# Seven block products in place of eight in a SwiGLU step, and a last stage laid out by tokens

## The chip, the cores and the metric

The kernel runs on one core of one Trainium2 chip. The metric is the device time of one execution in microseconds (us), here the median of three runs of the kernel before. The core has five engines with queues of their own: TensorE (PE in the profile, its weight loads PEld), VectorE (DVE), ScalarE (ACT), GpSimd (POOL) and SyncE (SP, which issues most DMAs).

## What is computed

One decoder layer on 512 tokens of width 1024, in float32: a SwiGLU half step, a mixer (attention beside a state-space model), a second SwiGLU half step, a gated embedding and a final norm. The change lies in the last three:

```python
h = h + 0.5 * swiglu(rmsnorm(h, g_ffn2), w1_b, w3_b, w2_b)
gate = sigmoid(rmsnorm(h, g_ple) @ w_ple_gate)
h = h + gate * (p @ w_ple_proj)
return rmsnorm(h, g_final)
# swiglu(x, w1, w3, w2) = (silu(x @ w1) * (x @ w3)) @ w2 ; w1, w3: 1024x2816, w2: 2816x1024
```

## The kernel before

The residual stream X lies transposed: eight tiles of 128 features x 512 tokens. A float32 product is made of three: every operand is split into hi (a cast to the type that PE reads) and lo = value - hi, and `mm3` (L235 to 238) issues hi*hi, lo*hi and hi*lo. So each weight piece of 128x512 passes through three engines before PE sees it: SP loads it into one of five raw buffers (`wdma`, L141), ACT casts it to hi and DVE subtracts (`split_w`, L152 to 168); the subtraction done, the raw buffer is free and the next load may start. A norm needs no pass of its own: the operand is X times the gain, and the factor 1/rms is applied behind the product (`Norm`, L254 on; its `chain` sums the squares on PE, takes the power on POOL and spreads the result by PE).

The work is a list of units of two steps each. `run` (L205) emits for each step, in this order: the hi casts of the next unit's weights, due evictions, chains, due posts, the lo subtractions, the step's matmuls. Every engine executes its queue in the order of emission, so this order is the schedule. `extra` asks for the conversion of a piece ahead of its unit.

The second FFN (`ffn_units`, L340; `U2`) has its 2816 hidden features in 22 tiles of 128, in three parts of 7, 7 and 8. For each tile there is one unit for the gate product (w1) and one for the linear product (w3): 8 blocks of the width x 3 matmuls with 512 tokens, 48 matmuls in the tile. Behind them `gate_a`, `gate_b`, `lin_a`, `lin_b`, `lin_c` (L348 to 368) make the hidden tile on DVE and ACT, with the tanh form of the sigmoid, and split it. After each part come eight w2 units that add the part's share onto X.

The projection of p (`proj_units`, L1222) is made in the mixer, as 8 tiles of features x tokens. The gate stage (`gate_units`, L1263) goes by output features: eight tiles m, and each in two halves of 256 tokens, so that the first half's final norm (`final_chain`, L1317) can run while the second half multiplies. Each unit has 24 matmuls with 256 tokens moving; behind them come the product with 1/rms, a tanh, the product with the projection, the sum onto X and a square. Twelve of the sixteen gate weight pieces are converted early, beside U2's units from the twentieth from the end on (L1418). After the last matmul `final_chain` sums the squares on PE, takes the power on POOL, spreads it over the partitions by PE, scales X by the gains into output tiles and sends them, six DMAs for the second half.

Of the kernel before, what the change touches and what calls it, by code (L numbers as in the profile page):

```python
# [23 lines left out]
PREP = 5  # L24
FEW = 3
# [5 lines left out]
OUT = [[(0, 1), (2, 3), (4, 5), (6, 7)], [(0,), (1, 2), (6,), (3, 4), (7,), (5,)]]  # L31
# [7 lines left out]
G_FFN1, G_MIX, G_FFN2, G_PLE, G_FINAL, G_ATTN, G_SSM, B_GLU = 0, 8, 16, 24, 32, 40, 44, 48  # L39
# [3 lines left out]
def hybrid_trunk_kernel(ctx: ExitStack, tc: tile.TileContext, xT, pT, w13a, w2a, w13b, w2b, wqk, wv, ws, wf,  # L43
                        wglu, wout, wgate, wproj, cols, bf, ssm_s, ssm_bc, dskip, outT, dbg=None):
# [48 lines left out]
    colt = const.tile([128, 52], F32, name="colt")  # L93
# [24 lines left out]
    qsel = [const.tile([128, L], F32R, name=f"qsel{j}") for j in range(2)]  # L118
    kcum = [const.tile([128, L], F32R, name=f"kcum{j}") for j in range(2)]
# [4 lines left out]
    class Unit:  # L124
# [6 lines left out]

        def w(self, c, n=1):
# [5 lines left out]
    wseq, raws = [], {}  # L138
    dma_at = [0]

    def wdma():  # L141
        j = dma_at[0]
        if j >= len(wseq):
            return
        dma_at[0] += 1
        u, i = wseq[j]
        n = u.srcs[i].shape[-1]
        w = pool.tile([128, 512], F32, name=nm("wraw"), tag="wraw", bufs=RAWS)
        nc.sync.dma_start(w[:, 0:n], u.srcs[i])
        raws[(id(u), i)] = w  # L150

    def split_w(u, i):  # L152
# [35 lines left out]
    def convert(u, nxt, h):  # L188
# [3 lines left out]
        if nxt is not None:  # L192
            res = [(nxt, i) for i in range(len(nxt.srcs)) if nxt.parts[i] is None and (i == h or last)]
        return res + [(v, i) for hh, v, i in u.extra if hh == h]

    def order_weights(units):
        seen = set()
        for u, nxt in zip(units, units[1:] + [None]):
            for h in range(len(u.steps)):
                for v, i in convert(u, nxt, h):  # L200
                    if (id(v), i) not in seen:
                        seen.add((id(v), i))
                        wseq.append((v, i))

    def run(units):  # L205
        while dma_at[0] < RAWS:
            wdma()
        for ui, u in enumerate(units):
# [3 lines left out]
            for h, step in enumerate(u.steps):  # L212
# [42 lines left out]
    class Norm:  # L255
# [52 lines left out]
        def chain(self, strided=False, wait=0):  # L308
# [12 lines left out]
            yield  # L321
            ps = bank()
# [899 lines left out]
    def proj_units(pp):  # L1222
# [270 lines left out]
    while chains:  # L1493
        advance(chains)
# [84 lines left out]
```

## Time and profile before

| | |
|---|---|
| median of 3 runs | 1009.3 us (1009.05 to 1009.88) |
| the profiled execution | 1009.63 us |
| its span, first to last instruction | 1007.9 us |
| busy: PE / DVE / ACT / POOL | 99% / 65% / 42% / 8% of the span |
| second FFN's parts 2 and 3, gate and linear tiles | 701.26 to 777.42 and 815.50 to 902.54 us |
| gate stage, then tail | 946.07 to 996.05, then to 1007.90 us |

Times in rows count from the span's start. A row's duration runs from an instruction's start to its end; those of one engine overlap, so the pace of an engine is read from the distance between two starts. "x2" behind a row of the timeline means two instructions merged, whose time is that of both together. POOL's durations are rough. An arrow names the output, then the inputs; buffer numbers are left out.

### The profile page before, as it was taken

To read this page: it belongs to the slowest core of one execution; us is meant where nothing else is said; L and a number is where in the kernel's file an instruction comes from. 1 tells how busy PE (TensorE), PEld (TensorE's weight loads), DVE (VectorE), ACT (ScalarE), POOL (GpSimd) and SP (SyncE) were. 2 spreads that over 40 slices of the span, in tenths; PEclk is the share of its full clock that TensorE was granted. 3 is DMA by queue.
4 is the path that set the end of the run, shared out by engine and by line. 5 is a ranking of instruction groups with operands and counts; after the bars stand their busy time and mean duration, and the time that the engine had idled before them with its cause. 6 is when DMAs were issued, how large, how long until landed. Compare 5 with 4: busy or idle time off the path is not lost.

```text
span 1007.9 us, 13796 instructions
## 1 busy us (share of the span) xinstructions
PE 996.2 (99%) x4980; PEld 838.5 (83%) x4980; DVE 655.1 (65%) x1297; ACT 420.7 (42%) x799; POOL 83.8 (8%) x84
## 2 busy tenths in 40 slices
PE   9999999999999999999999999999999999999996
PEld 7888888888878889887888888888888888888896
DVE  6668788767745565889987965543545347655465
ACT  6333233332244444469995543322333224434232
POOL 0440000001000001004651000000000000000000
PEclk9999999999999999999999999999999999999998
DMA  6423333223345323211212223233232334533102
GB/s 210 147 94 83 110 103 94 87 82 106 100 103 127 95 93 83 62 66 64 85 53 84 88 90 105 85 92 115 86 105 81 109 104 150 164 94 95 32 7 78
DMA packets 58244, 96.06 MB, mean 95 GB/s; under 512 B 10224, under 2 KB 17008, under 8 KB 58176
## 3 DMA queue, kind: packets, MB, share of 16 engines
q1 hardware_dynamic: 57920, 94.63, 31.0%
q8 instruction: 39, 0.64, 0.3%
q0 software_dynamic: 256, 0.56, 0.2%
q14 instruction: 29, 0.24, 0.1%
HBM read 91.89 MB, written 2.10 MB: 93 GB/s over the span
## 4 chain that ended last, share of the span: by engine, by line
PE 91%; DVE 5%; ACT 1%; issue 1%; DMA 1%; POOL 0%; SPq 0%; POOLq 0%; ACTq 0%; DVEq 0%
PE ps L236 29%; PE ps L238 29%; PE ps L237 28%; PE ps L1457 1%; PE ps L1093 1%; DVE rot L75 1%; DVE wlo L75 1%; DVE rc L75 1%; PE ps L324 1%; PE ps L1139 1%; PE ps L316 0%; PE ps L1138 0%; DMA x<-xT 0%; DVE qkhl L75 0%; PE ps L642 0%
## 5 line engine op out<-in xcount | busy, mean ns | idle before, releaser
L236 PE MATMUL ps<-xhl,whi 128*128 128x512 f32 x816 | 320.3, 393 | 0.0
L238 PE MATMUL ps<-xhl,whi 128*128 128x512 f32 x816 | 317.8, 389 | 0.0
L237 PE MATMUL ps<-xhl,wlo 128*128 128x512 f32 x816 | 317.7, 389 | 0.0
L160 ACT CAST whi<-wraw 128x512 fp32r<-128x512 f32 x324 | 195.9, 608 | 240.0 <-PE ps L238 176.9
L75 DVE TENSOR_TENSOR wlo<-wraw,whi 128x512 fp32r<-128x512 f32 x324 | 216.9, 675 | 5.8 <-ACT whi L160 5.5
L238 PEld LDWEIGHTS ps<-xhl,whi 128*128 128x128 f32 x816 | 153.2, 188 | 32.5
L236 PEld LDWEIGHTS ps<-xhl,whi 128*128 128x128 f32 x816 | 153.2, 188 | 31.8 <-issue 1.0
L237 PEld LDWEIGHTS ps<-xhl,wlo 128*128 128x128 f32 x816 | 153.3, 188 | 31.1
L236 PE MATMUL ps<-h,whi 128*128 128x512 f32 x352 | 137.3, 390 | 0.0
L238 PE MATMUL ps<-h,whi 128*128 128x512 f32 x352 | 137.0, 389 | 0.0
L237 PE MATMUL ps<-h,wlo 128*128 128x512 f32 x352 | 137.0, 389 | 0.0
L78 DVE SCALAR_TENSOR_TENSOR x<-ps,x 128x512 f32<-128x512 f32 x48 | 33.2, 692 | 95.1 <-PE ps L238 95.1
L78 DVE SCALAR_TENSOR_TENSOR t<-ps,rbc 128x512 f32<-128x512 f32 x44 | 30.4, 690 | 75.9 <-PE ps L238 75.9
L238 PEld LDWEIGHTS ps<-h,whi 128*128 128x128 f32 x352 | 66.1, 188 | 13.8
L237 PEld LDWEIGHTS ps<-h,wlo 128*128 128x128 f32 x352 | 66.1, 188 | 13.7
L236 PEld LDWEIGHTS ps<-h,whi 128*128 128x128 f32 x352 | 66.1, 188 | 13.5
L75 DVE TENSOR_TENSOR t<-ps,rbc 128x512 f32<-128x512 f32 x44 | 30.4, 691 | 71.1 <-PE ps L238 65.0
L81 ACT ACTIVATE th<-t 128x512 f32<-128x512 f32 x44 | 27.8, 632 | 91.0 <-DVE t L75 91.0
L364 ACT CAST h<-t 128x512 fp32r<-128x512 f32 x44 | 27.4, 622 | 80.9 <-DVE t L75 80.9
L320 POOL TENSOR_TENSOR rc<-ms,mhalf 128x4 f32<-128x4 f32 x6 | 8.0, 1338 | 519.6 <-DVE ms L319 519.6
L1085 POOL TENSOR_SCALAR lg<-lg,rs 128x128 f32<-128x128 f32 (+3 forms) x32 | 37.8, 1195 | 97.9 <-issue 78.7
L81 ACT ACTIVATE xhl<-x,colt 128x512 fp32r<-128x512 f32 x32 | 23.0, 725 | 48.1 <-DVE x L78 41.0
(256 smaller groups left out, 1185.0 us busy)
## 6 DMA issues: line engine op xcount, KB each, us to landing
wraw<-w13b SPq DMA_DIRECT2D x88, 256.0 KB, 2.9
wraw<-w13a SPq DMA_DIRECT2D x84, 256.0 KB, 2.8
wraw<-w2a SPq DMA_DIRECT2D x32, 256.0 KB, 2.7
wraw<-w2b SPq DMA_DIRECT2D x32, 256.0 KB, 2.7
wraw<-wqk SPq DMA_DIRECT2D x16, 256.0 KB, 2.8
wraw<-wout SPq DMA_DIRECT2D x16, 256.0 KB, 2.8
wraw<-wgate SPq DMA_DIRECT2D x16, 256.0 KB, 2.9
wraw<-w2a SPq DMA_DIRECT2D x16, 192.0 KB, 2.4
```

The lines of the kernel that those rows point to most:

```text
L75: V.tensor_tensor(out, a, b, op)
L78: V.scalar_tensor_tensor(out, a, s, b, op0, op1)
L81: S.activation(out, in_, f, **kw)
L160: S.copy(hi[:, 0:n], w[:, 0:n])
L236: T.matmul(ps, lh, rh, start=start, stop=False)
L237: T.matmul(ps, ll, rh, start=False, stop=False)
L238: T.matmul(ps, lh, rl, start=False, stop=stop)
L324: T.matmul(ps[:, i * 128:(i + 1) * 128], rc[:, i:i + 1].to_broadcast([128, 128]), ident, start=True, stop=True)
L364: S.copy(hl[:, 0, :], box["t"])
L1085: G.tensor_scalar(x, x, rs[h2][:, j:j + 1], None, MUL)
L1093: T.transpose(ps[:, j * 128:(j + 1) * 128], lg[h2][:, j * 128:(j + 1) * 128], ident)
L1139: T.matmul(po[:, j * 128:], vv, pl, start=False, stop=j == 3)
```

## The change

- In the second FFN, tiles 0 to 2 stay as they are (`PLAIN`). For each of the 19 others (`quick_units`) the two weight matrices are taken as a 2x2 block matrix, gate and linear by the two halves of the width, and X times gain as 2x2 blocks, halves of the width by halves of the tokens. Seven block products (of 4 blocks x 3 matmuls, 256 tokens moving) replace eight. Their stationary operands are the four raw pieces or sums of them; POOL makes four sums a tile, ACT casts and DVE subtracts seven operands of 128x512. The sums stand in buffers that attention has left (`spare`, `maskp`). The moving operands are X's halves and four combinations of them that `halves` makes once, on ACT, POOL and DVE, beside the plain tiles.
- The seven products are added up in three halves of two PSUM banks. Four intermediate sums are copied out by ACT (`p1`, `p5`, `u2`, `u3`) before the next product is added on. What follows (`gate_a` to `hid_b`) takes ten operations on DVE, ACT and POOL, two of them products with 1/rms on POOL (on DVE in the last tile of each part).
- The operands are taken five products ahead (`AHEAD`). A quick unit has seven steps; its loads wait for the raw buffers of the tile before, which POOL's third sum and DVE's subtractions free (`used`).
- The projection and the gate stage go by tokens: the activations are stationary (128 tokens), the weights move (512 output features). X is turned by PE (`turn`, four transposes for each half of a token tile). 1/rms is a column then and enters as the tanh's scale; the squares are summed by ACT's accumulator, and the final norm needs no product. Three token tiles leave as 512 KB each; the last half tile is made in two pieces (`last`) and leaves in two DMAs.
- The gate weights' subtractions stand on POOL, and twelve are converted beside the last eight w2 units. The final gains come by two DMAs on POOL's queue (`g_load`).

```diff
...
+PLAIN = (3, 0, 0)
...
+    rings = {"w": [], "k": []}
+    SIZE = {"w": RAWS, "k": 1}
     def wdma():
...
+        while dma_at[0] < len(wseq):
+            u, i = wseq[dma_at[0]]
+            ring = "k" if isinstance(u, Quick) and i == 3 else "w"
+            done = rings[ring]
...
+            if ring == "k":
+                w = spare(3)
+            else:
+                w = pool.tile([128, 512], F32, name=nm("wraw"), tag="wraw", bufs=RAWS)
+            nc.sync.dma_start(w[:, 0:n], u.srcs[i])
+            raws[(id(u), i)] = w
+    def used(u, i):
+        ring, j = where[(id(u), i)]
+        rings[ring][j] = True
+        wdma()
...
+            (G.tensor_tensor if u.alloc is not None else tt)(lo[:, 0:n], w[:, 0:n], raw32(hi[:, 0:n]), SUB)
+            used(u, i)
...
+    HT = L // 2
+    def halves(nrm, goff):
+        nrm.ta, nrm.tb = [None] * 4, [None] * 4
+        for _ in range(2):
+            yield
+        for k in range(4):
...
+            act(xa, X[k], AF.Copy, scale=colt[:, goff + k:goff + k + 1])
...
+            G.tensor_tensor(ta[:, 0:HT], xa[:, HT:], xa[:, 0:HT], SUB)
...
+            for _ in range(4):
+                yield
+            for t, dst in ((ta, nrm.ta), (tb, nrm.tb)):
+                hl = g4([128, 2, L], F32R, "xth")
+                S.copy(hl[:, 0, :], t)
+                dst[k] = hl
+                defer(1, lambda t=t, hl=hl: tt(hl[:, 1, :], t, raw32(hl[:, 0, :]), SUB))
+    def quick_units(nrm, w13, fs, hid, before):
+        A21, A22, A11, A12 = range(4)
+        KINDS, AHEAD = 7, 5
+        total = KINDS * len(fs)
+        tens = [Quick([w13[f, wi][:, c * 512:(c + 1) * 512] for wi, c in ((1, 0), (1, 1), (0, 0), (0, 1))]) for f in fs]
+        ops = {}
+        def first_sum(q):
+            G.tensor_tensor(spare(0), q.raw(A21), q.raw(A22), ADD)
+        def take(j):
+            n, i = divmod(j, KINDS)
+            q = tens[n]
+            def f():
+                src = (lambda: q.raw(A11), lambda: spare(0), lambda: maskp, lambda: q.raw(A12), lambda: spare(1), lambda: spare(2),
+                       lambda: q.raw(A22))[i]()
...
+                S.copy(hi, src)
+                ops[j] = hi, lo
+                if i == 0:
+                    G.tensor_tensor(maskp, spare(0), q.raw(A11), SUB)
+                elif i == 2:
+                    G.tensor_tensor(spare(1), q.raw(A11), q.raw(A21), SUB)
+                    used(q, A21)
+                    used(q, A11)
+                elif i == 3:
+                    G.tensor_tensor(spare(2), q.raw(A12), maskp, SUB)
+                elif i == 6 and n + 1 < len(fs):
+                    first_sum(tens[n + 1])
+                def rest():
+                    tt(lo, src, raw32(hi), SUB)
+                    if i == 3:
+                        used(q, A12)
+                    elif i == 6:
+                        used(q, A22)
+                return rest
+            return f
+        def moving(i, k, w):
+            lower, upper = slice(0, HT), slice(HT, L)
+            x, y = nrm.hl[k], nrm.hl[k + 4]
+            src, ts = ((x, lower), (nrm.ta[k], lower), (nrm.ta[k], upper), (y, lower), (nrm.tb[k], lower), (y, upper),
+                       (nrm.tb[k], upper))[i]
+            return src[:, w, ts]
+        before[-2].behind.extend((q, i) for q in tens for i in range(4))
+        before[-2].hooks.setdefault(1, []).append(lambda: first_sum(tens[0]))
+        for h, js in ((0, (0, 1)), (1, (2, 3, 4))):
+            before[-1].hooks.setdefault(h, []).extend(take(j) for j in js)
+        units = []
+        for n, f in enumerate(fs):
+            box = {}
+            def product(i, n=n, box=box):
+                def g(u):
+                    if i < 2:
+                        box[i] = bank()
+                    out = box[0][:, 0:HT] if i in (0, 2, 4, 6) else box[1][:, HT:] if i in (1, 5) else box[1][:, 0:HT]
+                    hi, lo = ops.pop(n * KINDS + i)
+                    for k in range(4):
+                        ks = slice(k * 128, k * 128 + 128)
+                        first = k == 0 and i < 2
+                        T.matmul(out, hi[:, ks], moving(i, k, 0), start=first, stop=False, skip_group_check=i > 1)
+                        T.matmul(out, lo[:, ks], moving(i, k, 0), start=False, stop=False, skip_group_check=i > 1)
+                        T.matmul(out, hi[:, ks], moving(i, k, 1), start=False, stop=k == 3, skip_group_check=i > 1)
+                return g
+            def p1(box=box):
+                box["t"] = tmp(base="t1")
+                S.copy(box["t"][:, 0:HT], box[0][:, 0:HT])
+            def p5(box=box):
+                box["u"] = tmp(base="t3")
+                S.copy(box["u"][:, 0:HT], box[1][:, HT:])
+            def u2(box=box):
+                S.copy(box["t"][:, HT:], box[0][:, 0:HT])
+            def u3(box=box):
+                S.copy(box["u"][:, HT:], box[0][:, 0:HT])
+            last = f == fs[-1]
+            MULT = tt if last else (lambda o, a, b, op: G.tensor_tensor(o, a, b, op))
+            def gate_a(box=box, MULT=MULT):
+                t = box["t"]
+                tt(t, box[1], t, ADD)
+                MULT(t, t, nrm.r, MUL)
+            def lin_a(box=box):
+                u = box["u"]
+                tt(u[:, HT:], u[:, HT:], u[:, 0:HT], ADD)
+            def gate_b(box=box):
+                box["h"] = tmp(base="th")
+                act(box["h"], box["t"], AF.Tanh, scale=0.5)
+            def gate_c(box=box, MULT=MULT):
+                stt(box["t"], box["h"], 1.0, box["t"], ADD, MUL)
+                MULT(box["t"], box["t"], nrm.r, MUL)
+            def lin_b(box=box):
+                h, t = box["h"], box["t"]
+                stt(h[:, HT:], box["u"][:, HT:], 0.5, t[:, HT:], MUL, MUL)
+                stt(h[:, 0:HT], box[0][:, 0:HT], 0.5, t[:, 0:HT], MUL, MUL)
+            def hid_a(box=box, f=f):
+                hl = g4([128, 2, L], F32R, "h")
+                S.copy(hl[:, 0, :], box["h"])
+                hid[f] = hl
+            def hid_b(box=box, f=f):
+                tt(hid[f][:, 1, :], box["h"], raw32(hid[f][:, 0, :]), SUB)
+            d = (0, 0, 0, 1, 1) if last else (0, 1, 2, 3, 4)
+            u = Unit([], [product(i) for i in range(KINDS)],
+                     [(0, 0, p1), (1, 0, p5), (2, 0, u2), (4, 0, u3), (5, 0, gate_a), (5, 0, lin_a)]
+                     + [(6, e, fn) for e, fn in zip(d, (gate_b, gate_c, lin_b, hid_a, hid_b))])
+            for i in range(KINDS):
+                j = n * KINDS + i + AHEAD
+                if j < total:
+                    u.hooks[i] = [take(j)]
+            units.append(u)
+        return units
...
+                if f - part[0] >= n_plain:
+                    units += quick_units(nrm, w13, list(part)[n_plain:], hid, units[-2:])
+                    break
...
+                    for t in (a, a + 1):
+                        ts = slice(t * 128, t * 128 + 128)
+                        box[t] = bank()
                         for k in range(2):
-                            mm3(box[mi], *u.w(mi * 2 + k), phl[k][:, 0, :], phl[k][:, 1, :], k == 0, k == 1)
+                            mm3(box[t], phl[k][:, 0, ts], phl[k][:, 1, ts], *u.w(k * 4, 4), k == 0, k == 1)
...
+        class Tile:
...
+            def turn(self, c):
+                ps = bank()
+                for j in range(4):
+                    T.transpose(ps[:, j * 128:(j + 1) * 128], X[c * 4 + j][:, self.t * 128:self.t * 128 + 128], ident)
+                return ps
+            def gate(self, ps, w):
+                th = tmp(base="gt")
+                act(th[:, 0:w], ps, AF.Tanh, scale=nrm.rc[:, 4 + self.t:5 + self.t])
+                return th
+            def add(self, th, px, c0, w):
...
+                o = self.o[:, c0:c0 + w]
+                stt(th[:, 0:w], th[:, 0:w], 1.0, pp[self.t][:, c0:c0 + w], ADD, MUL)
+                tt(o, th[:, 0:w], px, ADD)
+                act(th[:, 0:w], o, AF.Square, scale=1.0 / 32.0, accum_out=self.ss[:, self.n:self.n + 1])
...
+            def rms(self):
...
+                V.tensor_scalar(ms, ss[:, self.n - 1:self.n], ss[:, self.n - 2:self.n - 1], EPS, ADD, ADD)
+                G.tensor_tensor(rf, ms, mhalf[:, 0:1], ALU.pow)
...
+            def out(self):
+                for c in range(2):
+                    o = self.o[:, c * 512:(c + 1) * 512]
+                    stt(o, o, self.rf, gfb[c], MUL, MUL)
+                nc.sync.dma_start(y_out[self.t * 128:self.t * 128 + 128, :], self.o)
...
+        def products(u_of, ps, t, c, k0, k1, w0=0, w=512):
+            ts = slice(t * 128, t * 128 + 128)
+            for k in range(k0, k1):
+                xh, xl = nrm.pair(k)
+                hi, lo = ws_[c, k // 2].w((k % 2) * 4, 4)
+                mm3(ps[:, 0:w], xh[:, ts], xl[:, ts], hi[:, w0:w0 + w], lo[:, w0:w0 + w], k == 0, k == KD - 1)
...
+        def last():
+            tl = tiles[3]
+            px = tl.turn(1)
+            pss = [bank(), bank()]
             for i in range(2):
+                products(None, pss[i], 3, 1, 0, KD, i * 256, 256)
+                if i == 0:
+                    G.tensor_tensor(tl.o[:, 0:512], tl.o[:, 0:512], gfb[0], MUL)
+                th = tl.gate(pss[i][:, 0:256], 256)
+                tl.add(th, px[:, i * 256:i * 256 + 256], 512 + i * 256, 256)
+            tl.rms()
+            rows = y_out[384:512, :]
+            o = tl.o
+            stt(o[:, 512:1024], o[:, 512:1024], tl.rf, gfb[1], MUL, MUL)
+            nc.sync.dma_start(rows[:, 512:1024], o[:, 512:1024])
+            act(o[:, 0:512], o[:, 0:512], AF.Copy, scale=tl.rf)
+            nc.sync.dma_start(rows[:, 0:512], o[:, 0:512])
+        return units, load, last
...
-    chain_at(u_g[0], n4.chain(wait=1))
-    chain_at(u_g[KD], final_chain(acc5, sqs[0], 0, 3))
+    chain_at(U2[0], halves(n3, G_FFN2))
+    chain_at(u_g[0], n4.chain(wait=4, halved=True))
+    u_g[0].starts.append(g_load)
     for j in range(12):
-        U2[j // 2 - 20].extra.append((j % 2, u_g[j // 2], j % 2))
+        U2[j // 2 - 8].extra.append((j % 2, u_g[j // 2], j % 2))
...
```

## Rows read from the trace of the kernel before

**Rows 1.** The page: busy time of each engine, share of the span.
```profile
PE 996.2 (99%) x4980; PEld 838.5 (83%) x4980; DVE 655.1 (65%) x1297; ACT 420.7 (42%) x799; POOL 83.8 (8%) x84
```

**Rows 2.** Table of stretches: length, busy us by engine, clock, DMA share, GB/s.
```profile
701.26:777.42 76.16, 76.16 (x337) 63.08 (x336) 39.13 (x61) 24.69 (x41) 0.00 (x0) 1.00 0.31 95
815.50:902.54 87.04, 87.04 (x385) 72.10 (x384) 51.69 (x82) 35.19 (x59) 0.00 (x0) 1.00 0.44 133
946.07:996.05 49.98, 49.94 (x417) 49.64 (x416) 30.48 (x73) 15.91 (x36) 1.81 (x2) 1.00 0.07 22
996.05:1007.90 11.85, 3.64 (x22) 3.17 (x20) 4.30 (x11) 1.70 (x4) 2.10 (x3) 0.65 0.27 89
```

**Rows 3.** Timeline of PE (start, duration): transposes; matmuls around the norm sum.
```profile
478.30 1.04 PE L1093 MATMUL ps<-ident,lg 128*128 128x128 f32 x8
...
948.71 0.28 PE L237 MATMUL ps<-xhl,gw 128*128 128x256 f32 x1
948.83 0.29 PE L238 MATMUL ps<-xhl,gw 128*128 128x256 f32 x1
...
950.07 0.36 PE L236 MATMUL ps<-xhl,gw 128*128 128x256 f32 x1
```

**Rows 4.** Timeline of DVE, two consecutive operations in the second FFN.
```profile
881.59 0.68 DVE L75 TENSOR_TENSOR wlo<-wraw,whi 128x512 fp32r<-128x512 f32 x1
882.19 0.69 DVE L75 TENSOR_TENSOR t<-t,t 128x512 f32<-128x512 f32 x1
```

**Rows 5.** Groups by form, DVE and ACT: count, busy us, mean ns, idle.
```profile
L75 DVE TENSOR_TENSOR x<-x,gt 128x256 f32<-128x256 f32 x16 | 6.8, 425 | 0.5
L160 ACT CAST whi<-wraw 128x512 fp32r<-128x512 f32 x292 | 179.5, 618 | 204.5 <-PE ps L238 147.4 <-ACT whi L160 28.6 <-issue 18.1
L1109 ACT CAST pa<-ps 128x256 fp32r<-128x256 f32 x24 | 9.1, 379 | 2.3 <-PE ps L1093 2.3
```

**Rows 6.** Groups by form, POOL, one tensor input.
```profile
L1085 POOL TENSOR_SCALAR lg<-lg,rs 128x512 f32<-128x512 f32 x8 | 12.9, 1623 | 0.0
L1085 POOL TENSOR_SCALAR lg<-lg,rs 128x256 f32<-128x256 f32 x8 | 7.9, 990 | 0.0
```

**Rows 7.** Timelines, POOL and DVE: casts alone, casts beside DVE, that DVE, DVE alone.
```profile
385.41 1.27 POOL L1036 CAST qsel<-selr 64x512 fp32r<-64x512 f32 x2
...
469.86 2.12 POOL L1036 CAST qsel<-selr 64x512 fp32r<-64x512 f32 x2
...
469.81 1.70 DVE L75 TENSOR_TENSOR qkhl<-qk,kcum 64x512 fp32r<-64x512 f32 x2
...
478.45 1.40 DVE L75 TENSOR_TENSOR qkhl<-qk,qkhl 64x512 fp32r<-64x512 f32 x2
```

**Rows 8.** Timelines of POOL and DVE, a weight split beside two one-input operations.
```profile
490.04 3.10 POOL L1085 TENSOR_SCALAR lg<-lg,rs 128x512 f32<-128x512 f32 x2
...
491.73 1.08 DVE L75 TENSOR_TENSOR wlo<-wraw,whi 128x512 fp32r<-128x512 f32 x1
```

**Rows 9.** Timeline of all engines, the tail.
```profile
995.93 0.28 PE L238 MATMUL ps<-xhl,gw 128*128 128x256 f32 x1
...
996.25 0.42 DVE L75 TENSOR_TENSOR gt<-ps,rbc 128x256 f32<-128x256 f32 x1 [1.09 <-PE ps L238]
...
996.71 0.42 ACT L81 ACTIVATE gt<-gt 128x256 f32<-128x256 f32 x1 [1.03 <-DVE gt L75]
...
998.14 0.51 ACT L81 ACTIVATE xg<-x,colt 128x256 f32<-128x256 f32 x1 [0.61 <-DVE x L75]
...
999.50 0.70 POOL L1337 TENSOR_TENSOR rc<-ms,mhalf 128x2 f32<-128x2 f32 x1 [20.02 <-DVE ms L1336]
...
1002.82 1.41 POOL L1355 TENSOR_TENSOR o<-xg,r 128x256 f32<-128x256 f32 x2 [2.62 <-ACT r L1349]
```

**Rows 10.** DMA issues: weights (KB, us to landing); outputs (ns, starts).
```profile
wraw<-w13b SPq DMA_DIRECT2D x88, 256.0 KB, 2.9
...
L1358 SPq DMA_DIRECT2D outT<-o x10: 344/378/440, 981.3 to 1005.0; - x10
```

More of the change, by code (lines that the diff above doesn't have):

```diff
@@ L115, in hybrid_trunk_kernel, with spare_tile, spare @@
     selr = const.tile([128, 8], F32R, name="selr")
-    qsel = [const.tile([128, L], F32R, name=f"qsel{j}") for j in range(2)]
-    kcum = [const.tile([128, L], F32R, name=f"kcum{j}") for j in range(2)]
+    def spare_tile(dt, base):
+        return pool.tile([128, L], dt, name=nm(base), tag="spare", bufs=4)
+    qsel = [spare_tile(F32R, "qsel") for _ in range(2)]
+    kcum = [spare_tile(F32R, "kcum") for _ in range(2)]
+    spares = []
+    def spare(i):
+        if not spares:
+            spares.extend(spare_tile(F32, "sum") for _ in range(4))
+        return spares[i]
     HALF = [slice(0, 64), slice(64, 128)]
@@ L192, in convert @@
         if nxt is not None:
-            res = [(nxt, i) for i in range(len(nxt.srcs)) if nxt.parts[i] is None and (i == h or last)]
+            res = [(nxt, i) for i in range(len(nxt.srcs)) if nxt.parts[i] is None and (i == h - (len(u.steps) - 2) or last)]
         return res + [(v, i) for hh, v, i in u.extra if hh == h]
@@ L341, in ffn_units @@
+    def ffn_units(nrm, w13, w2, final, skip_first=False, plain=None):
         units = []
@@ L1271, in gate_units, with part @@
+        tiles = [Tile(t) for t in range(4)]
+        for t in range(4):
+            tl = tiles[t]
+            for c in range(2):
                 box = {}
-                def part(c, box=box, hs=hs, m=m):
+                def part(k0, k1, box=box, t=t, c=c, tl=tl):
                     def f(u):
-                        if c == 0:
-                            box[0] = bank()
-                        for k in range(c * 4, c * 4 + 4):
-                            xh, xl = nrm.pair(k)
-                            mm3(box[0][:, 0:H], *ws_[m].w(k), xh[:, hs], xl[:, hs], k == 0, k == KD - 1)
-                    return f
@@ new lines, in gate_units, with alloc @@
+                if c == 1:
+                    posts += [(1, 2, tl.rms), (1, 3, tl.out)]
+                if t == 3 and c == 1:
+                    continue
+                if t == 0:
+                    for kk in range(4):
+                        srcs = [wgate[2 * kk + i][:, c * 512:(c + 1) * 512] for i in range(2)]
+                        def alloc(box={"n": c * 8 + kk * 2}):
+                            box["n"] += 1
+                            return alloc_for(box["n"] - 1)()
+                        u = Unit(srcs, [part(2 * kk, 2 * kk + 1), part(2 * kk + 1, 2 * kk + 2)],
+                                 posts if kk == 3 else [], lambda: nrm.r is not None, alloc)
+                        ws_[c, kk] = u
+                        units.append(u)
+                else:
+                    units.append(Unit([], [part(0, 4), part(4, 8)], posts, lambda: nrm.r is not None))
```

206 lines of the change are left out of this document (86 added, 120 removed).

## The prediction

> **What bounds the kernel now.** I read the busy table first: PE is busy in 99% of the span and DVE in 65%, so the question is whether that PE time is dense or only looks so [rows 1]. The table of stretches, cut at the stages that the change touches, answers it: the second FFN's seven tiles of its middle part take 76.16 us and the eight of its last part 87.04 us, PE without a gap and at full clock, 10.88 us a tile in both [rows 2]. A tile is 48 matmuls of 512 columns, so one takes 0.227 us: nothing but PE's pace sets these stages. DVE works 39.13 of 76.16 us there, ACT 24.69, POOL nothing at all [rows 2]. The gate stage is PE as well: 49.98 us for 384 matmuls of 256 columns that start 0.12 us apart [rows 2, 3], plus pieces of two norm chains. Only the last 11.85 us are not PE's: the granted clock, a mean of its two levels, is down to 0.65 of the upper one there, and a chain of short steps runs through DVE, ACT, POOL and a DMA [rows 2].
>
> **What the seven products are worth to PE.** A quick tile is 7 products of 12 matmuls of 256 columns: 84 x 0.12 = 10.08 us, against 10.88. Most of the saved eighth is eaten by the shorter matmul: half the columns cost 0.53 of the time. For 19 tiles PE alone would save 19 x 0.80 = 15.2 us, if everything else fits into 10.08 us a tile.
>
> **What a quick tile asks of the others.** DVE: seven splits lo = src - hi, one product (h+1)*t and one split of the hidden tile (nine operations 512 wide), the sum of the halves of u and one half of the last product (two 256 wide). All eleven read two operands from SBUF; two more (gate_a's sum, the other half of the last product) read one from PSUM. Consecutive 512-wide operations start 0.60 us apart though each shows 0.69 [rows 4]; a 256-wide one shows 0.425 [rows 5], 0.265 less, so I count 0.34. That is 9 x 0.60 + 2 x 0.34 = 6.08 us with two SBUF inputs and 0.94 without. ACT: seven casts, a cast and a tanh at 0.62 and four half copies at 0.38 [rows 5], 7.1 us: no bound. POOL: four weight sums and two products with 1/rms, six operations of 128x512 with two inputs. The trace has none; the nearest is 128x256, 1.41 us for two [rows 9], so one of 512 lies between 0.70 + 0.63 = 1.33 (the one-input form's step from 256 to 512, 0.99 to 1.62 [rows 6]) and 2 x 0.70 = 1.40. Six are at most 8.4 us: by itself POOL fits too. In the last tile of each part the two products stand on DVE, 7.28 us for DVE and four operations for POOL.
>
> **But DVE and POOL do not run beside each other.** Two POOL casts of 64x512 take 1.27 us alone, and 2.12 us where two DVE subtractions with two SBUF inputs fall on them; the DVE pair takes 1.70 us, against 1.40 for the like form with POOL idle [rows 7]. A weight split grows to 1.08 us over POOL work [rows 8]. So the two take turns, and what counts is how long one POOL operation keeps DVE out (its hold). DVE, cast, DVE in 1.70 us, less 0.60 and 0.69, leaves 0.41 us for one input 512 wide; by the difference of the pairs it is 0.30. It is shorter than POOL's instruction: the split of 1.08 us is over at 492.81, while POOL's pair runs to 493.14 [rows 8]; under a hold to the end it could not have begun before that. For two inputs I take twice, 0.82 us; the bounds are 2 x 0.30 = 0.60 and the whole instruction, 1.33.
>
> [...]
>
> **The sum of the quick tiles.** Turns in series: 6.08 + 6 x 0.82 = 11.0 us for 16 tiles, 7.28 + 4 x 0.82 = 10.56 for the three last ones, 207.7 us against 19 x 10.88 = 206.7: +1.0 us. The 0.94 us of DVE without a second SBUF input lie under POOL's turns. PE would then wait 0.9 us a tile. The path to it: stationary operands are taken five products ahead (7 us), but three products add onto a PSUM half that ACT must first have copied, and ACT's casts of POOL's sums queue ahead of those copies.
>
> **What else moves.** The token sums (16 ACT operations, 16 POOL operations of 0.7 us, 8 DVE splits) fall into the three plain tiles, 32.6 us: DVE has 3 x 5.6 = 16.8 us there (39.13/7 of rows 2) and gets 5, POOL 11.2; even one after the other that is 33, and much of DVE's work there reads PSUM. Cost 0; without this cover POOL's 11 us. Sixteen splits of gate weights go to POOL, 16 x 1.33 = 21 us, twelve of them beside the last eight w2 units, 43 us long with DVE half idle: 0, else what DVE loses to them. On SP the tiles' DMAs now wait for POOL's third sum instead of a DVE split, with the next tile's operands queued behind; 256 KB land 2.9 us after issue [rows 10] and are wanted a tile later: 0. The last tile of a part needs some 4.2 us (six steps of 0.6 to 0.7) for its hidden pair, wanted 6.8 us on (30 matmuls of 0.227): 0. The projection keeps 48 matmuls of 512 columns: 0. Two DMAs on POOL's queue (g_final) stand ahead of the norm's power, which is wanted only when the first tile's gate is through, some 7 us on: 0.
>
> **Gate stage.** 168 x 0.227 + 48 x 0.12 = 43.9 us, one norm sum (1.24 us between the matmuls around it, 948.83 to 950.07) and 32 transposes of 0.11 (eight in 1.04 us with the last one's 0.27) [rows 3]: 48.6 us against 49.98, -1.4 us. The broadcast of 1/rms and the first final chain are gone.
>
> **Tail.** Before: last gate matmul to the end of the span, 995.93 to 1007.9, 11.97 us [rows 2, 9]. After, by the same kinds of steps: the first evacuation starts 0.32 on (now the tanh), its product, sum and square follow by 1.43 (996.71 to 998.14), so the square starts at 1.75; square 0.42 and its accumulator and two short DVE operations, some 0.75 in all, bring the power to 2.9 with its 0.3 of waiting; power 0.70, a 512-wide product 0.75, first DMA at 4.45, second 0.4 later, and 2.9 us from the last issue to the end (1005.0 to 1007.9): 7.75 [rows 9, 10]. That is -4.2 us; no broadcast through PE, no six outputs.
>
> **Total.** +1.0 - 1.4 - 4.2 = -4.6 us on the profiled execution's 1009.63 us, whose span is 1007.9; the median of the runs, 1009.3, is 0.3 lower, so 1004.7 us. With hold h the quick tiles cost 119.1 + 108 h us: 0.1 us of hold is 10.8 us, and h = 0.863 ends where the kernel stands today. This one term decides.
>
> **Rivals.** (1) PE stays the bound: under h = 0.667, 6.08 + 6 h is below 10.08 and the quick tiles take 191.5 us, -15.2 - 5.6: 988.5 us. For it: the difference of the pairs (0.60). Against: two engines would have to take turns with hardly an idle one. (2) Slower: POOL holds DVE out as long as it computes, at the quick tiles' six POOL operations. It decides from h = 0.863 on. Half-way from 0.82 to the whole instruction, h = 1.08, gives 16 x 12.56 + 3 x 11.6 = 235.8 us, +29.1 - 5.6: 1032.8 us; the whole 1.33 gives 1059.5. For it: the trace has no two-input POOL operation beside a DVE split, and these must be fed twice as much. Against: rows 8. (3) The turns hold but the last stage gives nothing, since its first units give PE 0.68 us of matmuls a step while POOL splits weights: 1010.3 us. Against: twelve of sixteen are split before it.
>
> **How the numbers follow.** Forecast (h from 0.70 to 0.93, 992 to 1016 us) 0.33; PE bound 0.30; longer hold 0.32; no gain in the last stage 0.05. About 0.2% (2 us) is what a measurement of this kernel tells from no change: h from 0.845 to 0.882. Of the forecast case 0.22 lie below that, 0.05 inside it, 0.06 above; with rival 3 inside: faster 0.52, same 0.10, slower 0.38. The forecast case alone is 992 to 1016; as cases of both signs weigh, the range goes from the PE bound to just over the half-way hold: 987 to 1035.
>
> **What would show it.** A quick tile in 11.0 us (10.1 for rival 1, 12.5 for rival 2); DVE's weight splits at 0.9 us mean instead of 0.69; POOL's 128x512 rows near 1.33 alone and 1.8 beside DVE; PE idle 0.9 us a tile ahead of the third, fifth or seventh product, ended by ACT's copy. Gate stage 48.6, tail 7.8. I am wrong if the splits keep 0.69 us, or if PE waits for something that DVE and POOL don't share.

## The result and the profile after

The kernel after takes 1063.15 us (median of four runs, 1061.95 to 1063.47), the kernel before 1009.55 beside it: a ratio of 1.0528, 95% interval 1.0513 to 1.0542. I had forecast 1004.7 us, in a range of 987 to 1035. The profiled execution spans 1061.4 us.

The first two lines are the page's busy times and the shares of the chain that ended last, both of the kernel after:

```profile
PE 998.7 (94%) x5484; PEld 862.2 (81%) x5484; DVE 764.7 (72%) x1326; ACT 475.7 (45%) x942; POOL 286.4 (27%) x227
...
PE 62%; issue 18%; DVE 9%; POOL 6%; ACT 3%; DMA 1%; SPq 0%; POOLq 0%; DVEq 0%; ACTq 0%
```

PE has lost its 99% [rows 1], and POOL has gone from 8% to 27% of the span. The table of stretches of the kernel after, with the columns of [rows 2]: the first quick tile, an ordinary one, the first of part 2, the gate stage and the tail:

```profile
core 0: us, PE busy (x) PEld busy (x) DVE busy (x) ACT busy (x) POOL busy (x), PEclk, DMA share, GB/s
620.50:640.90 20.40, 12.71 (x86) 12.17 (x85) 14.99 (x19) 6.88 (x15) 8.23 (x7) 0.83 0.25 79
655.04:669.21 14.17, 11.78 (x86) 11.58 (x85) 12.07 (x14) 6.16 (x13) 8.95 (x7) 0.88 0.27 83
718.98:729.02 10.04, 10.04 (x85) 10.03 (x84) 8.84 (x11) 5.75 (x12) 5.17 (x5) 1.00 0.34 107
1001.10:1053.20 52.10, 50.29 (x257) 41.00 (x256) 17.77 (x30) 14.18 (x30) 8.98 (x9) 1.00 0.08 31
1053.20:1061.40 8.20, 0.17 (x2) 0.00 (x0) 1.94 (x5) 1.70 (x4) 0.54 (x1) 0.68 0.18 65
```

The third row is the tile as PE alone would have it: 10.04 us, dense, at full clock. It is the first of its part and has no earlier tile whose hidden chain runs beside it. An ordinary one takes 14.17 us, and PE is busy in 11.78 of them, at a mean granted clock of 0.88. The 19 quick tiles, from the first matmul of each to the first of the next, come to 260.4 us, where the kernel before needs 206.7 for the same features. Against the forecast: tiles +52.7 us (207.7 was forecast), gate stage +3.5 (48.6), tail +0.45 (7.75), together 56.7 of 58.5 us. Of the other 1.8, some 0.9 lie in the projection of p, which goes by tokens now and for which I had put 0: it starts level with the kernel before (519.25 against 519.36 us), and the matmuls behind the mixer start 0.92 later (553.30 against 552.38). Its first unit waits for a weight split; what cost the rest of the 0.9 I did not take apart:

```profile
521.02 0.50 PE L275 MATMUL ps<-wlo,phl 128*128 128x512 f32 x1 [0.48 <-DVE wlo L75]
```

The waits of the kernel after, from the first quick tile to the gate stage (us in all, times, longest):

```profile
ACT h L525 <- DVE th L78: 59.6, 19, 3.5
ACT th L81 <- POOL t L499: 51.6, 16, 4.4
POOL t L499 <- DVE t L75: 48.2, 16, 8.9
POOL t L499 <- DVE t L78: 42.4, 16, 2.6
PE ps L479 <- ACT t L493: 36.4, 16, 2.6
DVE th L78 <- POOL t L499: 18.9, 16, 1.2
```

PE waits 16 times, once in every tile but the first of each part, for L493: `u2`, ACT's copy of the PSUM half onto which the fifth product adds. The other lines are one chain: DVE, POOL (L499, the product with 1/rms), ACT's tanh, DVE, POOL again, DVE, ACT's cast of the hidden tile (L525). The timeline shows it in one tile (start, duration, in brackets the idle time before and what ended it):

```profile
888.63 1.33 POOL L499 TENSOR_TENSOR t<-t,rbc 128x512 f32<-128x512 f32 x1 [2.50 <-DVE t L75]
888.74 1.77 DVE L75 TENSOR_TENSOR wlo<-sum,whi 128x512 fp32r<-128x512 f32 x1
890.00 0.63 ACT L81 ACTIVATE th<-t 128x512 f32<-128x512 f32 x1 [3.90 <-POOL t L499]
...
892.45 0.68 DVE L75 TENSOR_TENSOR wlo<-wraw,whi 128x512 fp32r<-128x512 f32 x1
892.61 1.68 POOL L499 TENSOR_TENSOR t<-t,rbc 128x512 f32<-128x512 f32 x1 [2.65 <-DVE t L78]
894.25 1.26 POOL L417 TENSOR_TENSOR sum<-wraw,wraw 128x512 f32<-128x512 f32 x1
894.32 1.47 DVE L78 SCALAR_TENSOR_TENSOR th<-t,t 128x256 f32<-128x256 f32 x1 [1.19 <-POOL t L499]
895.71 0.41 DVE L78 SCALAR_TENSOR_TENSOR th<-ps,t 128x256 f32<-128x256 f32 x1
...
896.21 0.62 ACT L525 CAST h<-th 128x512 fp32r<-128x512 f32 x1 [3.49 <-DVE th L78]
896.74 0.36 ACT L493 COPY t<-ps 128x256 f32<-128x256 f32 x1
897.16 0.38 PE L479 MATMUL ps<-xth,whi 128*128 128x256 f32 x1 [2.57 <-ACT t L493]
```

Two things are to be seen. First, the split at 888.74 takes 1.77 us where one alone shows 0.69: POOL started 0.11 us ahead of it and kept it out for 1.08. The half product at 894.32, 256 wide, takes 1.47 in place of the 0.41 of its fellow at 895.71; a POOL sum started 0.07 us ahead of it (894.25). That is the hold which I had put at 0.82. Second, the copy that PE wants stands behind the cast in ACT's queue, though its own data have been there since 893.2: the whole chain, with its two passes through POOL, stands ahead of PE's fifth product.

### The profile page after: what moved, and what is told of

It reads as the page before. It is cut to its first block, busy times and chain, and to the rows that moved or that the text cites. A ratio compares the mean times of both kernels' runs of the same rounds, so it can differ in the third digit from the quotient of the medians.

```text
span 1061.4 us, 15153 instructions
## 1 busy us (share of the span) xinstructions
PE 998.7 (94%) x5484; PEld 862.2 (81%) x5484; DVE 764.7 (72%) x1326; ACT 475.7 (45%) x942; POOL 286.4 (27%) x227
## 3 DMA queue, kind: packets, MB, share of 16 engines
q0 software_dynamic: 416, 1.08, 0.3%
## 4 chain that ended last, share of the span: by engine, by line
PE 62%; issue 18%; DVE 9%; POOL 6%; ACT 3%; DMA 1%; SPq 0%; POOLq 0%; DVEq 0%; ACTq 0%
PE ps L273 18%; PE ps L275 18%; PE ps L274 18%; POOL t L499 4%; DVE h L75 2%; DVE wlo L75 2%; DVE wq L75 2%; PE ps L479 2%; PE ps L481 1%; PE ps L480 1%; DVE t L75 1%; ACT h L525 1%; PE ps L1689 1%; DVE th L78 1%; PE ps L1299 1%
## 5 line engine op out<-in xcount | busy, mean ns | idle before, releaser
L196 ACT CAST whi<-wraw 128x512 fp32r<-128x512 f32 x248 | 148.3, 603 | 159.1 <-PE ps L275 116.8
L273 PE MATMUL ps<-xhl,whi 128*128 128x512 f32 x512 | 202.2, 395 | 0.0
L75 DVE TENSOR_TENSOR wlo<-wraw,whi 128x512 fp32r<-128x512 f32 (+1 forms) x269 | 195.8, 733 | 7.3 <-ACT whi L196 5.3
L275 PE MATMUL ps<-xhl,whi 128*128 128x512 f32 x512 | 199.7, 390 | 0.0
L274 PE MATMUL ps<-xhl,wlo 128*128 128x512 f32 x512 | 199.5, 390 | 0.0
L275 PEld LDWEIGHTS ps<-xhl,whi 128*128 128x128 f32 x512 | 96.2, 188 | 20.5
L273 PEld LDWEIGHTS ps<-xhl,whi 128*128 128x128 f32 x512 | 96.2, 188 | 20.0 <-issue 1.0
L274 PEld LDWEIGHTS ps<-xhl,wlo 128*128 128x128 f32 x512 | 96.3, 188 | 19.0
L273 PEld LDWEIGHTS ps<-h,whi 128*128 128x128 f32 x352 | 66.1, 188 | 13.5
L479 PE MATMUL ps<-xth,wq 128*128 128x256 f32 x156 | 47.4, 304 | 27.8 <-ACT t L493 18.8
L499 POOL TENSOR_TENSOR t<-t,rbc 128x512 f32<-128x512 f32 x32 | 48.5, 1516 | 90.6 <-DVE t L75 48.2
L479 PE MATMUL ps<-xth,whi 128*128 128x256 f32 x148 | 44.5, 301 | 18.7 <-ACT t L493 17.6
L479 PEld LDWEIGHTS ps<-xth,wq 128*128 128x128 f32 x156 | 31.3, 201 | 30.7 <-ACT t L493 20.6
```

Of the source, the lines that this page charges most:

```text
L75: V.tensor_tensor(out, a, b, op)
L196: S.copy(hi[:, 0:n], w[:, 0:n])
L273: T.matmul(ps, lh, rh, start=start, stop=False)
L274: T.matmul(ps, ll, rh, start=False, stop=False)
L275: T.matmul(ps, lh, rl, start=False, stop=stop)
L479: T.matmul(out, hi[:, ks], moving(i, k, 0), start=first, stop=False, skip_group_check=i > 1)
```

## The experiments

Two theories come from this. **T** (turns): each POOL operation keeps DVE out for some 1.2 us, so DVE and POOL in series set the tile. **Q** (queue): the price is the order on ACT, a chain ahead of the copies. The diffs are against the kernel after; the kernel before had 1009.5 to 1010.1 us beside all of them. Runs 1, 2, 5, 6, 9 and 10 are one execution each, the others medians of four to ten. Expectations call run 5 e6_order and run 8 e9_combined.

**1. The hidden chain's last two steps later.**

```diff
-            d = (0, 0, 0, 1, 1) if last else (0, 1, 2, 3, 4)
+            d = (0, 0, 0, 1, 1) if last else (0, 1, 2, 4, 5)
```

> Only the order on ACT is changed: the cast of the hidden tile goes one step later, so that the copy of the third product's sum (u2) no longer stands behind it. Theory Q (the stall of 2.6 us before the fifth product, and the half clock after it, are a queue matter: u2 waits behind a cast whose chain crosses POOL twice): quick tiles fall from 14.2 to 10.1 to 11 us, total about 1005 us. Theory T (DVE and POOL take turns with a hold of 1.2 us, 6.08 + 6 x 1.2 = 13.3 us a tile, whatever the order): tiles stay at 13.3 or above, the stall moves to another product, total about 1048 us or more.

1058.2 us, quick tiles 255.2 in all. PE no longer waits for `u2`, but for `p1` ahead of the third product, behind the tanh. Two waits of this kernel:

```profile
ACT th L81 <- POOL t L499: 70.6, 16, 5.5
...
PE ps L479 <- ACT t L486: 40.4, 14, 5.6
```

The second tile of each part falls to 10.6 to 10.9 us, those behind it take 13.6 to 16.0, the last one of a part left out: this one place in ACT's queue wasn't it.

**2. The products with 1/rms on DVE** in every tile; POOL keeps the four sums.

```diff
-            MULT = tt if last else (lambda o, a, b, op: G.tensor_tensor(o, a, b, op))
+            MULT = tt
```

> The two products with 1/rms stand on DVE in every tile; POOL keeps the four weight sums. Theory Q: the chain no longer crosses POOL, the hidden cast is early, the stall before the fifth product goes: tiles 10.1 to 10.9 us, total about 1005 us. Theory T: 7.28 + 4 x 1.2 = 12.1 us a tile, total about 1029 us.

1050.6 us, quick tiles 248.5, PE still waits 31.6 us ahead of the fifth product. Neither theory's figure came; T's 1029 was missed by far. Run 9 has the same work in a later order: 8.7 us of the miss (248.5 - 239.8) are ACT's order, and T's sum lacked terms.

**3. The four sums on DVE too**, so that POOL has nothing in the quick tiles.

```diff
-            G.tensor_tensor(spare(0), q.raw(A21), q.raw(A22), ADD)
+            tt(spare(0), q.raw(A21), q.raw(A22), ADD)
...
+            MULT = tt
```

> Nothing of a quick tile on POOL: products and the four sums on DVE. No turns, and no chain over POOL. Both theories: DVE's own work bounds the tile, 7.28 + 0.94 + 4 x 0.60 = 10.6 us, 19 tiles 202 us against 260 us; total about 1004 us. If it stays above 1030 us, neither holds and the couplings of PE and ACT alone cost the time.

1021.9 us, ratio 1.0117 (1.0099 to 1.0135); quick tiles 219.6, the ordinary one 11.7, with 1.45 us of PE's wait ahead of the fifth product. Six operations more on DVE, and 41 us less in the whole. The 10.6 us a tile that both theories gave were missed by 1.1; run 6 shows that half of this is the order.

**4. All 22 tiles plain**, no token sums: the new last stage alone.

```diff
-PLAIN = (3, 0, 0)
+PLAIN = (7, 7, 8)
...
-    chain_at(U2[0], halves(n3, G_FFN2))
```

> No quick tiles (all 22 as before, no token sums), the last stage by tokens as in the changed kernel. The traces say gate stage and tail together fell from 61.8 to 60.3 us: total about 1008 us by both theories. My prediction's sum, -5.6 us, would give 1004 us.

1009.0 us, ratio 0.9992 (0.9982 to 1.0002). The last stage, from which I had 5.6 us, gives next to nothing. The timeline of the gate stage of the kernel after shows where they went (this run shows the same waits):

```profile
1011.37 5.00 POOL L200 TENSOR_TENSOR gw<-wraw,gw 128x512 fp32r<-128x512 f32 x4 [4.47 <-ACT gw L196]
...
1012.70 0.51 PE L275 MATMUL ps<-gw,xhl 128*128 128x512 f32 x1 [0.63 <-POOL gw L200]
...
1013.94 0.50 PE L275 MATMUL ps<-gw,xhl 128*128 128x512 f32 x1 [0.26 <-POOL gw L200]
```

The last four gate pieces are converted just ahead of their matmuls, and POOL takes 1.25 us for a split (5.00 / 4) where the three matmuls of a piece need 0.68.

**5. Like 1, but the whole chain later**, behind the copies `p1`, `p5` and `u2`; POOL as in the kernel after.

```diff
-            d = (0, 0, 0, 1, 1) if last else (0, 1, 2, 3, 4)
+            d = (0, 0, 0, 1, 1) if last else (2, 3, 3, 4, 5)
```

> The changed kernel with all of the hidden chain's ACT work moved out of the way of the PSUM copies (tanh after the first copy, the hidden cast between the third and the fourth), POOL as it is. Shifting one cast alone only moved the stall from the fifth to the third product, so this tells order from turns. Theory Q2 (any ACT step of the chain ahead of a copy costs the stall, nothing else): quick tiles 10.1 to 11 us, total about 1005 us. Theory T (DVE and POOL in turns, hold 1.2 us): 13.3 us a tile at least on the long run, total 1045 us or more.

1053.0 us, quick tiles 250.3. PE now waits ahead of the seventh product, and the ordinary tile takes 13.6 us. With these three copies out of the way the turns show more plainly; `u3`, the copy that the seventh product needs, still stands behind the cast. From the timeline and the table of stretches of this run:

```profile
882.10 3.47 DVE L75 TENSOR_TENSOR wlo<-sum,whi 128x512 fp32r<-128x512 f32 x2
...
885.50 1.78 DVE L75 TENSOR_TENSOR wlo<-wraw,whi 128x512 fp32r<-128x512 f32 x1
...
889.90 1.47 DVE L78 SCALAR_TENSOR_TENSOR th<-t,t 128x256 f32<-128x256 f32 x1 [1.41 <-POOL t L499]
...
891.05 1.45 POOL L441 TENSOR_TENSOR sum<-sum,maskp 128x512 f32<-128x512 f32 x1
891.63 1.42 DVE L75 TENSOR_TENSOR wq<-sum,wq 128x512 fp32r<-128x512 f32 x1
```

```profile
909.54:923.14 13.60, 11.73 (x86) 11.53 (x86) 12.20 (x14) 6.17 (x13) 8.58 (x7) 0.88 0.23 77
```

DVE is busy 12.20 of 13.60 us, and the other 1.40 are its wait for POOL's second product. In the tile from 882 on, its pair at 882.10 lost 2.18 us to two POOL operations (3.47 against 1.29), the split at 885.50 1.09 to a third, the half product 1.06 to a fourth, the split at 891.63 0.73 to a fifth. The sixth, the second product, costs DVE no such loss but the 1.4 us in which DVE has nothing to do until its result is there. So DVE has hardly any slack left, five times for POOL's turn and once for its result, and T's 13.3 us a tile and 1045 us or more came; 14.17 - 13.6 is all that this change of ACT's order was worth in an ordinary tile.

**6. Order and no POOL**: the edits of 5 and 3 together.

```diff
-            G.tensor_tensor(spare(0), q.raw(A21), q.raw(A22), ADD)
+            tt(spare(0), q.raw(A21), q.raw(A22), ADD)
...
+            MULT = tt
...
+            d = (0, 0, 0, 1, 1) if last else (2, 3, 3, 4, 5)
```

> The same order, and nothing of a quick tile on POOL. Without POOL the tiles took 11.7 us with a stall of 1.6 us behind the hidden cast. If that stall is order alone, DVE's work is left as the bound: 10.6 to 10.8 us a tile, total about 1010 us. If PE still waits 1.6 us a tile, DVE's backlog itself delays the chain: 1020 us.

1010.7 us, quick tiles 207.6. The ordinary tile takes 11.15 us and what the six POOL operations cost in the sum of the tiles is 250.3 - 207.6 = 42.7 us.

**7. Run 4 with the gate's subtractions on DVE** and its last four pieces converted earlier.

```diff
-            (G.tensor_tensor if u.alloc is not None else tt)(lo[:, 0:n], w[:, 0:n], raw32(hi[:, 0:n]), SUB)
+            tt(lo[:, 0:n], w[:, 0:n], raw32(hi[:, 0:n]), SUB)
...
+    for j in range(12, 16):
+        u_g[j // 2 - 5].extra.append((j % 2, u_g[j // 2], j % 2))
```

> All tiles plain, last stage by tokens, with the gate weights' subtractions on DVE and the last four pieces converted beside the gate stage's second and third unit. With POOL the stage lost about 3.5 us to these four pieces (52.1 us against the 48.6 counted). If that is the whole loss, the total falls from 1009.0 to about 1005.5 us; if the last stage has another cost, it stays at 1008 to 1009 us.

1005.5 us, ratio 0.996 (0.9946 to 0.9974). The last stage by tokens is worth 4 us with these two edits. Both the engine and the time of the last four splits change here, so the run does not part them.

**8. What the runs point to, together**: the edits of 6, those of 7 to the gate, and a fourth plain tile (`PLAIN = (4, 0, 0)`) to cover the token sums.

```diff
-PLAIN = (3, 0, 0)
+PLAIN = (4, 0, 0)
...
```

> Order and no POOL as above, four plain tiles first in place of three (the first quick tile paid 5 us for DVE's backlog from the token sums), and the gate pieces as in the run before. By both: 18 tiles x 10.7 + 10.9 us = 203.5 us against 206.7 before, minus 5 us in the last stage: about 1001 us. If DVE's backlog persists: 1008 us or more.

1002.1 us, ratio 0.9925 (0.991 to 0.9939), faster than both kernels.

**9. Run 5 with the two products on DVE**: four POOL operations a tile in place of six, in the late order.

```diff
+            MULT = tt
...
+            d = (0, 0, 0, 1, 1) if last else (2, 3, 3, 4, 5)
```

> The chain later (as in e6_order) and the two products with 1/rms on DVE in every tile; POOL keeps the four weight sums. Theory T (turns: every two-input POOL operation keeps DVE out for 1.2 us): 7.28 + 4 x 1.2 = 12.1 us a steady tile in place of 13.6, so 16 x 1.5 = 24 us less than e6_order: 1029 us, 1024 to 1034. Rival R (the hidden chain's two passes through POOL cost all of it, the sums lie beside other work): 11.15 us a tile as with no POOL at all, 1014 us or less. Rival S (the sums cost all of it): 13 us or more, above 1043.

1042.6 us, quick tiles 239.8, the ordinary one of parts 2 and 3 13.1 us on average: T's 12.1 was too low, and these are the figures that S had named. S's cause does not hold all the same: taking the two products off POOL is worth 10.5 us of the tiles (250.3 - 239.8). POOL's and DVE's timelines, and the table of stretches over two tiles of this run:

```profile
904.42 1.67 POOL L437 TENSOR_TENSOR sum<-wraw,wraw 128x512 f32<-128x512 f32 x1 [2.90 <-DVE wq L75]
906.06 1.75 POOL L441 TENSOR_TENSOR sum<-sum,maskp 128x512 f32<-128x512 f32 x1
...
904.86 3.50 DVE L75 TENSOR_TENSOR wlo<-wraw,whi 128x512 fp32r<-128x512 f32 x2
...
911.74 1.24 DVE L75 TENSOR_TENSOR wq<-maskp,wq 128x512 fp32r<-128x512 f32 x1 [0.66 <-ACT wq L432]
```

```profile
sum 26.40, PE 22.08 PEld 21.68 DVE 24.87 ACT 12.26 POOL 12.55; mean PE 11.04 PEld 10.84 DVE 12.44 ACT 6.13 POOL 6.27
```

Two splits take 3.50 us in place of 1.29: 1.10 for each of the two sums. DVE is busy 24.87 of 26.40 us, so it still sets the pace. The sum T had used leaves out what DVE does with PSUM, 0.94 us a tile, and 0.66 in which it waits for an ACT cast (911.74): 7.28 + 0.94 + 0.66 + 4 h = 13.2 gives h = 1.08. The loss is about that of run 5, though a single one can be smaller (0.55 at 911.74); it was the other terms that failed.

**10. One input in place of two**: run 5, with the four sums as copies on POOL.

```diff
-            G.tensor_tensor(spare(0), q.raw(A21), q.raw(A22), ADD)
+            G.tensor_scalar(spare(0), q.raw(A22), 1.0, None, MUL)
...
```

> As e6_order (six POOL operations a tile), but each of the four weight sums is a copy of one of its operands times 1.0 on POOL, 128x512 with one input in place of two; the second operand is left out of the product. Theory T with the hold by inputs that the prediction read from rows 7 (one input keeps DVE out 0.41 us, two inputs 1.2): 6.08 + 4 x 0.41 + 2 x 1.2 = 10.1 us, so the tile is at the floor that the chain's order leaves, some 11.2 us, and the time 1012 to 1020 us. Rival L (a POOL operation keeps DVE out as long as it computes, with one input as with two: 1.3 us or more): 13.6 us a tile or more, 1050 us or above.

1017.3 us, quick tiles 213.6 in place of 250.3, the ordinary one 11.6. From this run's timeline, POOL's rows, then DVE's:

```profile
878.98 1.34 POOL L499 TENSOR_TENSOR t<-t,rbc 128x512 f32<-128x512 f32 x1 [1.96 <-DVE t L75]
880.29 1.92 POOL L417 TENSOR_SCALAR sum<-wraw 128x512 f32<-128x512 f32 x1
...
879.08 1.79 DVE L75 TENSOR_TENSOR wq<-sum,wq 128x512 fp32r<-128x512 f32 x1
880.79 1.09 DVE L75 TENSOR_TENSOR wlo<-sum,whi 128x512 fp32r<-128x512 f32 x1
```

The groups of POOL by shape, the first copy in this run, then the first sum in the kernel after (busy us, mean ns, idle time before):

```profile
L417 POOL TENSOR_SCALAR sum<-wraw 128x512 f32<-128x512 f32 x19 | 34.7, 1829 | 74.4 <-DMA wraw<-w13b 71.0 <-DVE t L75 3.3
```

```profile
L417 POOL TENSOR_TENSOR sum<-wraw,wraw 128x512 f32<-128x512 f32 x19 | 25.5, 1341 | 76.5 <-DMA wraw<-w13b 75.3 <-DVE wq L75 1.3
```

Beside the two-input product of 1.34 us the DVE split loses 1.10 us; beside the one-input copy, which lasts 1.92, it loses 0.40. The first copy takes 1.83 us on average where the sum took 1.34, and yet the kernel is 36 us faster than run 5. The copies leave out the second operand, so this kernel does not compute the layer; it is here for its time alone. What DVE lost here went by POOL's inputs, not by the length of its instruction. (The operation's form changes with the inputs, from a sum to a product with 1.0; that the one-input casts of [rows 7] gave 0.41 speaks for the inputs.) The expectation says that the prediction had read 1.2 us for two inputs; it had 0.82, and 1.2 is T's.

**11. Run 8 with the cast behind the copy**, the last wait that it showed (0.9 us ahead of the seventh product, in nine tiles; the expectation has 1.05 in ten).

```diff
-            d = (0, 0, 0, 1, 1) if last else (2, 3, 3, 4, 5)
+            d = (0, 0, 0, 1, 1) if last else (2, 3, 3, 6, 7)
```

> As e9_combined, but the hidden tile's cast (ACT) and its split come two steps later, behind ACT's copy u3 that PE's seventh product waits for; in e9_combined PE waits 1.05 us there in ten tiles (11.15 us a tile). Theory Q (the wait is only ACT's order): the wait goes, the eighteen quick tiles come to 10.05 us, and the time falls by 10 us to 992 us. Rival D (DVE is the next bound: 11 + 6 operations without any POOL are 6.08 + 0.94 + 6 x 0.60 = 10.62 us a tile): 10.6 to 10.8 us a tile in the steady ones, 996 to 999 us. If neither the order nor DVE were it, 1002 us stay.

996.2 us, ratio 0.9865 (0.9847 to 0.9883), the fastest of all. The ordinary tile of run 6, then two tiles of this run, in the table of stretches:

```profile
861.03:872.18 11.15, 10.26 (x86) 10.05 (x85) 10.99 (x21) 6.28 (x13) 0.00 (x0) 1.00 0.30 92
```

```profile
851.10:861.10 10.00, 10.00 (x86) 10.00 (x85) 9.90 (x18) 5.89 (x13) 0.00 (x0) 1.00 0.34 105
872.06:883.04 10.98, 10.53 (x87) 10.12 (x85) 10.88 (x20) 6.34 (x14) 0.00 (x0) 1.00 0.34 97
```

Both expectations are seen one after the other: up to five tiles go at PE's 10.0 us, with DVE falling behind, and when its slack is used up the tile is DVE's, 10.98 us, with no POOL at all.

## Why the prediction was wrong

**The step that failed is the hold.** The view of the mechanism was right: DVE and POOL take turns, and one term decides. From rows 7 I had 0.41 us for one input, and run 10 shows 0.40. "For two inputs I take twice, 0.82 us" was the guess. In most of the cases above DVE lost 1.06 to 1.10, four fifths of POOL's 1.33. But that is no length of its own: it depends on when DVE comes. What is the same each time is when DVE gets to work, counting 0.69 us for a 512-wide operation alone and 0.41 for a 256-wide one: 0.14 us before POOL's recorded end, at 888.74 (1.08 lost, 0.11 us behind POOL's start) as at 891.63 of run 5 (0.73 lost, 0.58 behind). In the kernel after, from its second quick tile to the gate stage, it is between 0.12 and 0.15 us in all 84 DVE operations of these two widths that take over 0.15 us longer than alone. With two inputs, then, POOL keeps DVE out for all but its whole instruction, the upper bound that I had put aside on the strength of rows 8; those show one-input operations and say nothing of two. With one input DVE gets to work 1.02 us before the copy's end (run 10). Rival 2's half-way value, 1.08, was the right mean, by luck: it stood there as a mid-point. Its 1032.8 us lacks the terms that follow.

**The second failed term: "0.94 us lie under POOL's turns".** That a DVE operation with an operand in PSUM takes no turn with POOL was my assumption; none of the rows that I gave shows it. For the smaller one the kernel after does: in 13 tiles it takes 0.41 us beside a POOL sum (at 895.71, 0.12 us behind the start of one of 1.33 us), as it does with POOL idle (951.40). The larger, 0.60, can't lie there: it is what POOL's first product waits for (2.50 us of idle time at 888.63 above), so POOL is idle while DVE does it. 6.08 + 0.94 + 6 x 1.09 = 13.56 us, and run 5 shows 13.6; the 1.09 fits as a mean only, since one of the six is the wait of 1.40 and one a loss of 0.73. These two terms make 2.6 us in an ordinary tile, of 3.2 lost against the 11.0 forecast; the remaining 0.6 are the order on ACT.

**The order.** I had named the coupling (a PSUM half that ACT must copy first, behind casts of POOL's sums) and let it carry the 0.9 us a tile that the turns leave, nothing beside them. The cast that stands ahead of the copy is that of the hidden tile, whose chain goes through POOL twice. In the sum of the tiles the ladder is: order 260.4 to 250.3 (run 5), two products off POOL 239.8 (run 9), four sums off POOL 207.6 (run 6). Each sum on POOL costs 32.2 / 76 = 0.42 us more than on DVE, so with DVE's own 0.60 it takes 1.02 us of DVE's time to spare 0.60. I had looked for the hold at which the whole change breaks even (0.863); the question for each operation was whether its hold is under 0.60.

**The low clock** stands beside PE's waits. In the first quick tile PE waits 5.59 us, and the matmuls after it start 0.21 us apart, not 0.12, at a granted clock of 0.50. The timeline of that tile, with a DVE row from just before it:

```profile
618.35 2.89 DVE L75 TENSOR_TENSOR xth<-xt,xth 128x512 fp32r<-128x512 f32 x2
...
631.55 0.58 PE L479 MATMUL ps<-xth,wq 128*128 128x256 f32 x1 [5.59 <-ACT t L486]
...
631.93 0.42 PE L480 MATMUL ps<-xth,wq 128*128 128x256 f32 x1
...
632.15 0.42 PE L481 MATMUL ps<-xth,wq 128*128 128x256 f32 x1
```

The granted clock from 631.55 to 634.00 is 0.50. The traces of both kernels show it at 1.00 or at 0.50: the mean of 0.65 in the tail before is 1.00 up to 999.5 us and 0.50 from 1000.0 on. In the quick tiles of the kernel after it is 0.50 in ten stretches, 6.8 us long in the first tile and 3.4 in the others. Each starts during a wait of PE of 2.3 us or more or within 1.5 us of its end, but behind four waits as long (2.48 to 2.58 us, up to 780.40, 794.61, 882.94 and 897.16) it stays at 1.00. What the low clock costs by itself stays open. In the kernel after, the tiles with at most two such matmuls average 13.5 us (four of them) and those with twelve or more 14.4 (nine); but a short tile is followed by a longer one, so the difference, 0.9 us a tile, holds both, and the rows do not part them.

**"Token sums: cost 0"** was wrong too. The first quick tile takes 20.35 us, 6 more than an ordinary one. DVE reaches it late, with splits of the token sums still to do at 618.35 (2.89 us for two, 1.29 elsewhere) and five stationary operands to take. I had spread DVE's 5 us and POOL's 11 evenly over the three plain tiles, and left out the first quick tile's own sums and splits, which fall there too. DVE's work is not even: it is busy 7.54, 9.21 and 10.89 us in the three, and has nothing left in the last:

```profile
609.70:620.59 10.89, 10.89 (x50) 9.02 (x48) 10.89 (x11) 6.62 (x12) 9.38 (x8) 1.00 0.26 82
```

With no POOL in the quick tiles the first one takes 16.4 us (run 6), with a fourth plain tile as well 11.6 (run 8).

**The last stage.** Gate 52.1 us in place of 48.6: "sixteen splits on POOL: 0" failed. It is rival 3 in small, at the last four pieces and not, as I put it, at the first units; runs 4 and 7 differ by 3.5 us, as much as the whole miss, and the stage itself goes from 52.2 to 49.0. The tail came nearly as worked out, 8.2 for 7.75. (Two slips in the sums change nothing: the tail's steps put the first DMA at 4.35 us and not 4.45, and h = 1.33 gives 1059.7 us.)

**What held**: 10.08 us for PE's own tile (10.04); POOL's 1.33 us, and up to 1.77 beside DVE; that PE's wait ends with ACT's copy. Rival 1 was right on PE, but only where POOL is out of the way (10.00 us a tile at 851.10 of run 11).

## What to carry to other kernels

Before an operation is moved to a second engine to spare the first, set what it takes from the first there against what it costs here: a two-input sum on POOL kept DVE out for up to 1.1 us and spared it 0.6. Work that both engines do alternately goes into one sum, and so does what either must do while the other waits. And where PE adds onto a buffer that another engine first copies out, look for the longest chain that stands ahead of the copy in that engine's queue.

## What the hardware showed that I had not expected

- A POOL copy of 128x512 (one input, 1.92 us) cost the DVE split beside it 0.40 us, a POOL product of the same size (two inputs, 1.34 us) 1.10 us. With two inputs DVE got to work 0.12 to 0.15 us before POOL's recorded end, in 84 of 84 cases of the kernel after; with one input 1.02 us before it (run 10).
- POOL loses as well, where DVE starts first: its product takes 1.33 to 1.35 us in the 15 places of the kernel after where it is 0.10 to 0.12 us ahead of DVE's split (888.63), and 1.65 to 1.68 in the 17 where a split has been running for 0.16 or 0.17 us (892.61).
